# The first mixer of a hybrid two-layer network without plain float32 products, and its zero blocks written first

## The chip, the cores and the metric

One core of one Trainium2 chip runs the whole program. The metric is the device time of one execution in microseconds. The kernel before has a median of 1746.74 us over three runs.

## What is computed

Two layers on one sequence of 256 rows of width 1024, all in float32. Each layer normalises x, projects it with w_in (1024 x 5024), feeds three branches from parts of the projection, gates and merges them, projects with w_out and adds to x; then comes a feed-forward part (layer 0 dense, layer 1 with eight experts of which each row takes two).

```python
h = rmsnorm(x, norm_mix[layer])
z = h @ w_in[layer]
cq, ckv, kpe, u_ssm, conv_a, conv_g, gates = jnp.split(z, IN_OFFSETS, axis=-1)
y_attn = mla_branch(cq, ckv, kpe, ...) @ w_o_attn[layer]
s = jax.nn.gelu(s5_branch(u_ssm, ...))
s = s * jax.nn.sigmoid(s @ ssm_w_glu[layer] + ssm_b_glu[layer])
y_ssm = s @ w_o_ssm[layer]
y_conv = conformer_conv_branch(conv_a, conv_g, ...) @ w_o_conv[layer]
g = jax.nn.sigmoid(gates).reshape(B, L, 3, D)
merged = g[:, :, 0] * y_attn + g[:, :, 1] * y_ssm + g[:, :, 2] * y_conv
x = x + merged @ w_out[layer]
```

## The kernel before, in words

**Weights and products.** Weights come from memory in units of 1 MB on SyncE's queue (`load_next`, two raw buffers) and are used in pieces of 128x1024. A piece holds the 128x128 blocks of eight products. `top_up` makes a piece ready: as a rule `split` writes a rounded high half with ScalarE (L198, `bwh`) and the difference as a low half with VectorE (L199, `bwl`), three buffers of each. `mm3` then does a product in three passes, high x high (L211), high x low (L212), low x high (L213), with the activations split in the same way (`aH`, `aL`). A piece whose key is "native" is handed on unsplit, and `mm3` does one product in plain float32 (L209), with unsplit activations (`h`, written by eight ScalarE copies, L737, in `to_hT`).

**The order of the first mixer.** A plan for each layer, a string in `CFG`, lists the projections (u, cq, conv, gate, ...) and, after a "+", the lanes that begin there (the tables of the state-space branch, its scan `ssm_gen`, the attention, the norm of the convolution). A "!" marks a native projection. Between the pieces `tick` gives the lanes their turns from a budget of VectorE time; each split takes 1.13 from it, each piece done adds to it (3.4 if native, otherwise 2.6). So fewer native pieces also move the lanes' steps in the order. A scheduler then fixes the order on each engine, except on GpSimd, which follows the program text.

**Names at the places that the change touches.** `setup` loads x and makes the identity; `feature_rows` loads nine small vectors (norm gains, biases), the first two on SyncE's queue and the other seven on GpSimd's; `rms` squares x on ScalarE (L668, `junk`) and makes nr, the inverse root, on VectorE (L133 and L136); `norm_stats` scales x to xn (L710, L711); L728 are the transposes. `ssm_tiles` makes the blocks mout0, mout1, bx with zeros around their content and writes the zeros with GpSimd (L537), `ssm_inp` does so for toep (L594). In the state-space branch rn and ab are blocks of coefficients, P (two tiles, hr and hi in the code) are the states after the scan, L1185 to L1187 the products of y with toep and mout, L1259 the transposes of ys in `ssm_act`, which then updates u (through lt). `cacc` is the sum of the convolution's taps, rr the inverse root of its norm, L762 spreads rr over rows, and br is the branch output that w_o_conv multiplies.

```python
if native:
    self.ready.append((key, src, None))
else:
    self.budget -= 1.13
    self.ready.append((key,) + self.wsplit(src))
```

Of the kernel before, what the change touches and what calls it, by code (L numbers as in the profile page):

```python
# [8 lines left out]
F32 = mybir.dt.float32  # L9
# [13 lines left out]
NCH = 16  # L23
# [14 lines left out]


CFG = dict(  # L40
    plans=("u0 u1! cq0 +out conv0! +in gate2! +tables +ssm ckv0 gate4! +norm gate0 gate5 gate7! conv1 "
           "qkv0 +attn gate6 glu0 ossm0 gate1 oattn0 gate8 ossm1 +cln gate3 gatea gateb oattn1 gate9 "
           "oconv0 oconv1",
           "u0 u1 +ssm gate5 cq0 conv0 gate6 gate7 ckv0 +norm gate4! glu0 conv1 qkv0 +attn ossm0 gate2 "
           "gate0 ossm1 gate1 gate8 +cln gatea oattn0 gate9 gate3 oattn1 gateb oconv0 oconv1"),
    rate=(1.0, 1.3), cap=(7.0, 3.0, 1.5), frate=0.85, native=("glu", ""), acc=("sc o b c", "b c sc o"),
    ngate=5, nraw=2, nwp=3, ns=3, wps="w w w aH",
    raw2="E mout0 mout1 U+v toep q cqk+zc k br br lc", raw3="bx+u mt,ys+P0,P1")

# [32 lines left out]
class Prog:  # L82
# [259 lines left out]
    def setup(self):  # L342
        nc, io = self.nc, self.io
        cp = self.cp = self.pool("const")
        self.mixp = self.pool("mix")
        self.nraw, self.nwp = CFG["nraw"], CFG["nwp"]
        self.raws, self.turn = [("raw", self.nraw)] * self.nraw, 0
        self.dr = self.pool("dr", space=bass.MemoryType.DRAM)
        self.x = cp.tile([128, 2, D], F32, name="x")
        for t in range(2):  # L350
            nc.sync.dma_start(self.x[:, t, :], io["x"][0, t * 128:(t + 1) * 128, :])
        self.ident = cp.tile([128, 128], F32, name="ident")
        make_identity(nc, self.ident)
        self.ones = cp.tile([128, 128], F32, name="ones")
        nc.vector.memset(self.ones, 1.0)
        self.lc, self.lc_at = self.mixp.tile([128, 2048], F32, name="lc", bufs=1), 0
        self.cmask = self.const(256)
        nc.gpsimd.memset(self.cmask, 0.0)
        nc.gpsimd.affine_select(self.cmask[:, 128:], self.cmask[:, 128:], pattern=[[-1, 128]],
                                compare_op=OP.is_ge, fill=-3.0e38, base=0, channel_multiplier=1)  # L360


    def feature_rows(self):
        nc, io = self.nc, self.io
        spec = [("norm_mix", 8), ("norm_ffn", 8), ("q_norm", 2), ("kv_norm", 1), ("ssm_d", 4),
                ("ssm_b_glu", 4), ("conv_b", 4), ("conv_ln_g", 4), ("conv_ln_b", 4)]
        rows = [self.mixp.tile([128, 128], F32, tag=t, name="frows", bufs=1) for t in ("wr", "P1")]
        self.col = {}
        r = 0
        for name, n in spec:  # L370
            first = r < 32
            (nc.sync if first else nc.gpsimd).dma_start(
                rows[0][r:r + 2 * n] if first else rows[1][r - 32:r - 32 + 2 * n],
                io[name].rearrange("l (c p) -> (l c) p", p=128))
            for l in range(DEPTH):
                self.col[name, l] = r + l * n
            r += 2 * n
        self.nf = r
        self.fv = self.cp.tile([128, r], F32, name="fv")
        return rows  # L380
# [149 lines left out]
    def ssm_tiles(self):  # L530

        wk = self.mixp
        self.mout = [wk.tile([128, NCH, Q, 2, 16], F32, name=f"mout{i}", bufs=1) for i in range(2)]
        self.bx = wk.tile([128, 2, 4, Q, 2, 16], F32, name="bx", bufs=1)
        self.E = wk.tile([128, 2, NCH, NQ], F32, name="E", bufs=1)
        for t in (self.bx, *self.mout):
            self.nc.gpsimd.memset(t, 0.0)  # L537


# [46 lines left out]
    def ssm_inp(self, l, ps):  # L586
        nc, io, wk = self.nc, self.io, self.mixp
        c0 = 16 * l
        c0m = self.c0m
        sh = [128, Q, 16, 16]  # L590
        flat = lambda v: v.rearrange("p k c o -> p (k c o)")
        self.minT = [wk.tile([128, NCH, 128], F32, tag=t, name="minT", bufs=1) for t in "qk"]
        toep = self.toep = wk.tile([128, NCH, 128], F32, name="toep", bufs=1)
        nc.gpsimd.memset(toep, 0.0)  # L594
        z = wk.tile([128, 2048], F32, tag="br", name="pz", bufs=2)
        tmp = z[:, :1024].rearrange("p (k c o) -> p k c o", k=Q, c=16)
        b = z[:, 1024:1536].rearrange("p (i c o) -> p i c o", i=2, c=16)
        for i, nm in enumerate(("ssm_b_re", "ssm_b_im")):
            nc.scalar.dma_start(b[:, i], io[nm][l].rearrange("(c g) p i -> (g p) c i", g=2))
        ab = wk.tile([128, 2, Q, 16, 16], F32, tag="br", name="ab", bufs=2)  # L600
        fr, fi = (self.bp[:, i].rearrange("p (k c) -> p k c", k=Q)[:, :, c0:c0 + 16, None].to_broadcast(sh) for i in range(2))
        br, bi = (b[:, i][:, None].to_broadcast(sh) for i in range(2))
        for o, x, y, op in ((0, br, bi, OP.subtract), (1, bi, br, OP.add)):
            self.tt(ab[:, o], fr, x, OP.mult)
            yield 1.1
            self.tt(tmp, fi, y, OP.mult)
            yield 1.1
            self.tt(flat(ab[:, o]), flat(ab[:, o]), flat(tmp), op)
            yield 1.1
        fx = lambda v: v.rearrange("p k g i -> p (k g i)")  # L610
        for u in range(4):
            cs = slice(4 * u, 4 * u + 4)
            for i in range(2):
                for d in range(2):
                    hp = slice(64 * d, 64 * d + 64)
                    nc.scalar.activation(self.bx[hp, i, :, :, d], ab[hp, i, :, cs].rearrange("p k c o -> p c k o"),
                                         AF.Copy)
            for i in range(2):
                p = self.spare(ps)
                for j in range(4):  # L620
                    nc.tensor.transpose(p[:, j * 128:(j + 1) * 128], fx(self.bx[:, i, j]), self.ident)
                nc.scalar.activation(self.minT[i][:, cs].rearrange("p a b -> p (a b)"), p, AF.Copy)
            p = self.spare(ps)
            for j in range(4):
                for i in range(2):
                    nc.tensor.matmul(p[:, 32 * j:32 * j + 32], fx(self.bx[:, i, j]),  # L626
                                     c0m[:, i, 4 * u + j].rearrange("p a b -> p (a b)"), start=(i == 0), stop=(i == 1))

            nc.scalar.activation(self.toep[:, cs, 96:], p[:, :128].rearrange("p (c m) -> p c m", c=4), AF.Copy)
            yield 0.5  # L630
        for st in range(Q - 1):
            for k in range(st + 1):
                o = 32 * (k + Q - 1 - st)
                nc.scalar.activation(self.toep[o:o + 32, :, 32 * st:32 * st + 32],
                                     self.toep[32 * k:32 * k + 32, :, 96:], AF.Copy)
        yield 0
# [223 lines left out]
    def mixer(self, l, wk, psp):  # L860
        nc, io = self.nc, self.io
# [435 lines left out]

        if l == 0:
            self.conv_params(psp)
            self.ssm_tiles()  # L1300
        lanes = dict(tables=lambda: self.ssm_tables(l), out=lambda: self.ssm_out(l, psp),
                     norm=attn_norm, attn=attn_gen, ssm=ssm_gen, cln=conv_ln)
        lanes["in"] = lambda: self.ssm_inp(l, psp)
# [2 lines left out]
        for tok in self.plan[l]:  # L1306
# [5 lines left out]
            t, e = tok.rstrip("!"), "!" * tok.count("!")  # L1312
            name, i = t[:-1], int(t[-1], 16)
# [600 lines left out]
```

## Time and profile before

| what | value |
|---|---|
| runs | 1746.73, 1746.74, 1750.08 us; median 1746.74 |
| profiled execution | 1745.99 us, span 1744.3 us |
| granted TensorE clock | 0.992 of full speed |
| TensorE (PE) busy | 1695.3 us, 97% |
| VectorE (DVE) busy | 1466.3 us, 84% |
| ScalarE (ACT) busy | 1169.5 us, 67% |
| GpSimd (POOL) busy | 48.5 us, 3% |

The span lies between the first and the last instruction of the profiled execution; 1.7 us of its time lie around it. The mixer of layer 0, which the change touches, ends at about 275 us of the span.

### The profile page before, as it was taken

The numbers are of one execution on the slowest core, as the hardware profiler recorded it, in microseconds if no ns is written. First come the engines' busy times: TensorE is split into PE (matmuls) and PEld (weight loads), VectorE is DVE, ScalarE is ACT, GpSimd is POOL, SyncE is SP. The second block draws the span as 40 slices with busy tenths as digits, with TensorE's granted clock in tenths as the row PEclk, the third lists the DMA queues.
The fourth block names the chain that finished last, engine by engine and source line by source line (L and its number), as shares of the span: only waits on it lengthen the run. The fifth ranks groups of instructions, "written<-read, shape, count | busy, mean of one in ns | idle before, by whom it ended". The sixth has DMA issues, their size and how long they took to land.

```text
span 1744.3 us, 26025 instructions
## 1 busy us (share of the span) xinstructions
PE 1695.3 (97%) x9687; PEld 1459.0 (84%) x9687; DVE 1466.3 (84%) x2150; ACT 1169.5 (67%) x1534; POOL 48.5 (3%) x71
## 2 busy tenths in 40 slices
PE   6999999999989999999999999999999999999997
PEld 5899898999979989978888888888788888888875
DVE  7878887855558997689999999989898988998897
ACT  4545555664453565567888887777777877878785
POOL 3000000000000000000000000000000000100020
PEclk9999999999999999989999999999999999999998
DMA  5433355545643756769999899799999899898993
GB/s 156 128 103 98 99 182 191 171 145 186 194 145 116 236 163 218 259 219 382 374 366 393 292 341 398 268 394 396 337 394 394 305 393 395 326 394 326 396 394 141
DMA packets 261899, 471.27 MB, mean 270 GB/s; under 512 B 26932, under 2 KB 104916, under 8 KB 261764
## 3 DMA queue, kind: packets, MB, share of 16 engines
q1 hardware_dynamic: 244580, 455.69, 73.2%
q0 software_dynamic: 2544, 8.06, 1.3%
q10 hardware_dynamic: 14640, 5.77, 1.3%
q8 instruction: 78, 1.28, 0.3%
q14 instruction: 57, 0.47, 0.1%
HBM read 463.70 MB, written 5.78 MB: 269 GB/s over the span
## 4 chain that ended last, share of the span: by engine, by line
PE 90%; DVE 5%; ACT 3%; DMA 2%; issue 1%; ACTq 0%; SPq 0%; DVEq 0%
PE mm L212 18%; PE mm L211 18%; PE mm L213 18%; PE Y L212 6%; PE Y L213 6%; PE Y L211 6%; PE acc L213 2%; PE acc L212 2%; PE acc L211 2%; PE mm L209 2%; PE tr L1709 1%; DVE bwl L199 1%; PE bu L1176 1%; PE spare L626 1%; ACT bwh L198 1%
## 5 line engine op out<-in xcount | busy, mean ns | idle before, releaser
L199 DVE TENSOR_TENSOR bwl<-braw,bwh 128x1024 fp32r<-128x1024 f32 x246 | 298.6, 1222 | 112.0 <-ACT bwh L198 103.9
L198 ACT ACTIVATE bwh<-braw 128x1024 fp32r<-128x1024 f32 x246 | 258.9, 1058 | 198.5 <-PE mm L212 121.8
L211 PE MATMUL mm<-bwh,bxm 128*128 128x512 f32 x672 | 266.1, 396 | 0.0
L212 PE MATMUL mm<-bwl,bxm 128*128 128x512 f32 x672 | 264.6, 394 | 1.2 <-DVE bwl L199 1.2
L213 PE MATMUL mm<-bwh,bxm 128*128 128x512 f32 x672 | 262.6, 391 | 0.0
L212 PEld LDWEIGHTS mm<-bwl,bxm 128*128 128x128 f32 x672 | 126.3, 188 | 33.5 <-DVE bwl L199 9.4
L211 PE MATMUL mm<-aH,bwh 128*128 128x256 f32 x528 | 153.1, 291 | 0.5 <-ACT bwh L198 0.5
L213 PE MATMUL mm<-aH,bwl 128*128 128x256 f32 x528 | 150.5, 285 | 1.4 <-DVE bwl L199 1.4
L212 PE MATMUL mm<-aL,bwh 128*128 128x256 f32 x528 | 150.6, 285 | 0.0
L213 PEld LDWEIGHTS mm<-bwh,bxm 128*128 128x128 f32 x672 | 126.1, 188 | 25.8
L211 PEld LDWEIGHTS mm<-bwh,bxm 128*128 128x128 f32 x672 | 126.3, 188 | 25.2
L212 PE MATMUL Y<-bwl,bgates 128*128 128x512 f32 x336 | 133.5, 397 | 0.8 <-DVE bwl L199 0.8
L213 PE MATMUL Y<-bwh,bgates 128*128 128x512 f32 x336 | 132.8, 395 | 0.0
L211 PE MATMUL Y<-bwh,bgates 128*128 128x512 f32 x336 | 122.5, 400 | 0.0
L136 DVE SCALAR_TENSOR_TENSOR cacc<-zc,lc,cacc 128x256 f32<-128x256 f32 x240 | 108.0, 478 | 3.4 <-ACT cacc L966 2.3
L211 PEld LDWEIGHTS mm<-aH,bwh 128*128 128x128 f32 x528 | 101.6, 193 | 4.1 <-issue 2.2
L213 PEld LDWEIGHTS mm<-aH,bwl 128*128 128x128 f32 x528 | 101.5, 192 | 1.8 <-DVE bwl L199 1.6
L212 PEld LDWEIGHTS mm<-aL,bwh 128*128 128x128 f32 x528 | 101.6, 192 | 0.2
L212 PE MATMUL mm<-fL,bwh 128*128 128x256 f32 x352 | 99.3, 282 | 0.0
L213 PE MATMUL mm<-fH,bwl 128*128 128x256 f32 x352 | 99.3, 282 | 0.0
L211 PE MATMUL mm<-fH,bwh 128*128 128x256 f32 x352 | 99.3, 282 | 0.0
L213 PE MATMUL mm<-baH,bxm 128*128 128x512 f32 x224 | 87.7, 392 | 0.0
(427 smaller groups left out, 4201.5 us busy)
## 6 DMA issues: line engine op xcount, KB each, us to landing
bmout<-in_moe_w SPq DMA_DIRECT2D x46, 1024.0 KB, 10.6
bbr<-in_moe_w SPq DMA_DIRECT2D x44, 1024.0 KB, 14.0
braw<-in_moe_w SPq DMA_DIRECT2D x44, 1024.0 KB, 14.2
braw<-in_w_in SPq DMA_DIRECT2D x38, 1024.0 KB, 5.4
braw<-in_ffn_w SPq DMA_DIRECT2D x31, 1024.0 KB, 5.4
bE<-in_moe_w SPq DMA_DIRECT2D x23, 1024.0 KB, 10.5
btoep<-in_moe_w SPq DMA_DIRECT2D x23, 1024.0 KB, 13.0
bq<-in_moe_w SPq DMA_DIRECT2D x23, 1024.0 KB, 14.2
```

What stands on the lines that cost most here:

```text
L136: self.nc.vector.scalar_tensor_tensor(out, a, s, b, op0=op0, op1=op1)
L198: i = nc.scalar.activation(h, src, AF.Copy)
L199: j = nc.vector.tensor_tensor(l, src, h.bitcast(F32), op=OP.subtract)
L209: mm(out, wh, xh, start=start, stop=stop, skip_group_check=True)
L211: mm(out, wh, xh, start=start, stop=False, skip_group_check=True)
L212: mm(out, wh, xl, start=False, stop=False, skip_group_check=True)
L213: self.lastmm = mm(out, wl, xh, start=False, stop=stop, skip_group_check=True).ins
L626: nc.tensor.matmul(p[:, 32 * j:32 * j + 32], fx(self.bx[:, i, j]), c0m[:, i, 4 * u + j].rearrange("p a b -> p (a b)"), start=(i == 0), sto ...
L1176: nc.tensor.matmul(pb[:, i, c], self.minT[i][:, pair_at(8 * h + c)], U[:, 8 * h + c], start=True, stop=True)
L1709: nc.tensor.transpose(p[:, q * 128:(q + 1) * 128], s[:, q * 128:(q + 1) * 128], self.ident)
```

## The change

Four things are done. The "!" is taken from all projections of layer 0 (u1, both parts of conv0, gates 2, 4 and 7), and "glu" from the native keys of layer 0, so that 14 pieces more are split and 112 products more go in three passes; the one native projection of layer 1 (gate4) stays. `ssm_tiles` is called in `setup`, right behind the identity, and also makes and clears toep of layer 0, in the order mout0, mout1, bx, toep. The last seven small vectors of `feature_rows` are loaded from ScalarE's queue. With no native piece in layer 0, the eight ScalarE copies of h go, and the output of the state-space branch is split for the product with the glu weights (two splits of 128x512 more).

```diff
--- before.py
+++ after.py
@@ -38,12 +38,12 @@
 
 
 CFG = dict(
-    plans=("u0 u1! cq0 +out conv0! +in gate2! +tables +ssm ckv0 gate4! +norm gate0 gate5 gate7! conv1 "
+    plans=("u0 u1 cq0 +out conv0 +in gate2 +tables +ssm ckv0 gate4 +norm gate0 gate5 gate7 conv1 "
            "qkv0 +attn gate6 glu0 ossm0 gate1 oattn0 gate8 ossm1 +cln gate3 gatea gateb oattn1 gate9 "
            "oconv0 oconv1",
            "u0 u1 +ssm gate5 cq0 conv0 gate6 gate7 ckv0 +norm gate4! glu0 conv1 qkv0 +attn ossm0 gate2 "
            "gate0 ossm1 gate1 gate8 +cln gatea oattn0 gate9 gate3 oattn1 gateb oconv0 oconv1"),
-    rate=(1.0, 1.3), cap=(7.0, 3.0, 1.5), frate=0.85, native=("glu", ""), acc=("sc o b c", "b c sc o"),
+    rate=(1.0, 1.3), cap=(7.0, 3.0, 1.5), frate=0.85, native=("", ""), acc=("sc o b c", "b c sc o"),
     ngate=5, nraw=2, nwp=3, ns=3, wps="w w w aH",
     raw2="E mout0 mout1 U+v toep q cqk+zc k br br lc", raw3="bx+u mt,ys+P0,P1")
 
@@ -351,6 +351,7 @@
             nc.sync.dma_start(self.x[:, t, :], io["x"][0, t * 128:(t + 1) * 128, :])
         self.ident = cp.tile([128, 128], F32, name="ident")
         make_identity(nc, self.ident)
+        self.ssm_tiles()
         self.ones = cp.tile([128, 128], F32, name="ones")
         nc.vector.memset(self.ones, 1.0)
         self.lc, self.lc_at = self.mixp.tile([128, 2048], F32, name="lc", bufs=1), 0
@@ -369,7 +370,7 @@
         r = 0
         for name, n in spec:
             first = r < 32
-            (nc.sync if first else nc.gpsimd).dma_start(
+            (nc.sync if first else nc.scalar).dma_start(
                 rows[0][r:r + 2 * n] if first else rows[1][r - 32:r - 32 + 2 * n],
                 io[name].rearrange("l (c p) -> (l c) p", p=128))
             for l in range(DEPTH):
@@ -533,7 +534,8 @@
         self.mout = [wk.tile([128, NCH, Q, 2, 16], F32, name=f"mout{i}", bufs=1) for i in range(2)]
         self.bx = wk.tile([128, 2, 4, Q, 2, 16], F32, name="bx", bufs=1)
         self.E = wk.tile([128, 2, NCH, NQ], F32, name="E", bufs=1)
-        for t in (self.bx, *self.mout):
+        self.toep = wk.tile([128, NCH, 128], F32, name="toep", bufs=1)
+        for t in (*self.mout, self.bx, self.toep):
             self.nc.gpsimd.memset(t, 0.0)
 
 
@@ -590,8 +592,9 @@
         sh = [128, Q, 16, 16]
         flat = lambda v: v.rearrange("p k c o -> p (k c o)")
         self.minT = [wk.tile([128, NCH, 128], F32, tag=t, name="minT", bufs=1) for t in "qk"]
-        toep = self.toep = wk.tile([128, NCH, 128], F32, name="toep", bufs=1)
-        nc.gpsimd.memset(toep, 0.0)
+        if l:
+            self.toep = wk.tile([128, NCH, 128], F32, name="toep", bufs=1)
+            nc.gpsimd.memset(self.toep, 0.0)
         z = wk.tile([128, 2048], F32, tag="br", name="pz", bufs=2)
         tmp = z[:, :1024].rearrange("p (k c o) -> p k c o", k=Q, c=16)
         b = z[:, 1024:1536].rearrange("p (i c o) -> p i c o", i=2, c=16)
@@ -1297,7 +1300,6 @@
 
         if l == 0:
             self.conv_params(psp)
-            self.ssm_tiles()
         lanes = dict(tables=lambda: self.ssm_tables(l), out=lambda: self.ssm_out(l, psp),
                      norm=attn_norm, attn=attn_gen, ssm=ssm_gen, cln=conv_ln)
         lanes["in"] = lambda: self.ssm_inp(l, psp)
```

Three places of the order, each before and after. First VectorE in the tables of the state-space branch (pz, rn and ab are its blocks of coefficients, c0m a small matrix, cacc the convolution's taps, `bwl` a low half of a weight piece). Before:

```order
L127 TENSOR_TENSOR rn<-pz,lc 128x1024 x2
L136 SCALAR_TENSOR_TENSOR c0m<-aux,lc 128x512
L127 TENSOR_TENSOR pz<-pz,lc 128x1024
L127 TENSOR_TENSOR rn<-rn,pz 128x1024
L127 TENSOR_TENSOR pz<-pz,lc 128x1024
L136 SCALAR_TENSOR_TENSOR rn<-rn,pz 128x1024
L136 SCALAR_TENSOR_TENSOR zc<-mt,zc 128x2x256
L136 SCALAR_TENSOR_TENSOR cacc<-zc,lc,cacc 128x256 x5
L127 TENSOR_TENSOR ab<-lc,pz 128x1024
L136 SCALAR_TENSOR_TENSOR cacc<-zc,lc,cacc 128x256
L199 TENSOR_TENSOR bwl<-braw,bwh 128x1024 x2
```

After (another `bwl` stands eight rows ahead of the first one shown; five short rows and two cacc lie between):

```order
L136 SCALAR_TENSOR_TENSOR c0m<-aux,lc 128x512
L127 TENSOR_TENSOR lc<-scr 128x32
L127 TENSOR_TENSOR pz<-pz,lc 128x1024
L127 TENSOR_TENSOR rn<-pz,lc 128x1024 x2
L127 TENSOR_TENSOR rn<-rn,pz 128x1024
L136 SCALAR_TENSOR_TENSOR cacc<-zc,lc,cacc 128x256
L127 TENSOR_TENSOR pz<-pz,lc 128x1024
L136 SCALAR_TENSOR_TENSOR cacc<-zc,lc,cacc 128x256
L136 SCALAR_TENSOR_TENSOR rn<-rn,pz 128x1024
L136 SCALAR_TENSOR_TENSOR cacc<-zc,lc,cacc 128x256
L199 TENSOR_TENSOR bwl<-braw,bwh 128x1024
```

The same operations stand in both, in nearly the same order; before, TensorE works on plain products meanwhile and the next `bwl` pair comes behind the first ab, while now these rows lie between one `bwl` and the next, and each piece that TensorE uses needs one.

Second, VectorE at the end of the scan of h = 1 (P as above, u and lt of the update in `ssm_act`, sm of the softmax). Before:

```order
L127 TENSOR_TENSOR P_1602<-wr,E 128x512
L127 TENSOR_TENSOR P_1603<-wr,E 128x512
L127 TENSOR_TENSOR P_1602<-P_1602,T_1604 128x512
L127 TENSOR_TENSOR P_1603<-P_1603,wi 128x512
L136 SCALAR_TENSOR_TENSOR u<-u,fv,aux 128x256 x2
L1118 ISA sm,st<-sc,lc 128x128
```

After:

```order
L127 TENSOR_TENSOR P_1827<-wr,E 128x512
L127 TENSOR_TENSOR T_1829<-wi,E 128x512
L136 SCALAR_TENSOR_TENSOR u<-u,fv,aux 128x256 x2
L127 TENSOR_TENSOR P_1827<-P_1827,T_1829 128x512
L127 TENSOR_TENSOR P_1828<-wr,E 128x512
L136 SCALAR_TENSOR_TENSOR lt<-lt,u 128x512
L127 TENSOR_TENSOR wi<-wi,E 128x512
L1121 ISA sm,st<-sc,lc 128x128
L1121 ISA st 128x1
L136 SCALAR_TENSOR_TENSOR u<-lt,u 128x512
L127 TENSOR_TENSOR P_1828<-P_1828,wi 128x512
```

Both P were whole ahead of the update of u; the second P is now finished behind it.

Third, TensorE at the end of the convolution's norm (aux spreads rr; br is a branch output, aH the normed input). Before, where br is still that of the attention:

```order
L211 MATMUL mm<-br,bwh 128x256
L212 MATMUL mm<-br,bwh 128x256
L762 MATMUL aux<-ident,rr 128x128 [waits DVE_49,PE_49]
L762 MATMUL aux<-ident,rr 128x128
L213 MATMUL mm<-br,bwl 128x256
L211 MATMUL mm<-br,bwh 128x256
L212 MATMUL mm<-br,bwh 128x256
L213 MATMUL mm<-br,bwl 128x256
```

After, where br is that of the convolution:

```order
L211 MATMUL mm<-aH,bwh 128x256
L212 MATMUL mm<-aL,bwh 128x256
L765 MATMUL aux<-ident,rr 128x128 [waits DVE_49,PE_49]
L765 MATMUL aux<-ident,rr 128x128
L213 MATMUL mm<-aH,bwl 128x256
L211 MATMUL mm<-br,bwh 128x256 [waits PE_49,Activation_49]
L211 MATMUL mm<-br,bwh 128x256 [waits Activation_49]
L212 MATMUL mm<-br,bwh 128x256 [waits DVE_49]
```

Before, 88 rows lie between the spreading of rr and the first product with the convolution's br; after, one row does.

## Rows read from the trace of the kernel before

**Rows 1.** The page, busy time of each engine.

```profile
PE 1695.3 (97%) x9687; PEld 1459.0 (84%) x9687; DVE 1466.3 (84%) x2150; ACT 1169.5 (67%) x1534; POOL 48.5 (3%) x71
```

**Rows 2.** Stretch 16 to 270 us: length, busy of PE, PEld, DVE, ACT, POOL; clock, DMA.

```profile
16.00:270.00 254.00, 249.65 (x1839) 228.35 (x1840) 217.39 (x575) 134.10 (x252) 4.26 (x8) 1.00 0.43 125
```

**Rows 3.** What TensorE waited for, 16 to 290 us: total, times, longest.

```profile
PE hp L728 <- ACT xn L710: 8.3, 1, 8.3
PE mm L213 <- DVE bwl L199: 1.4, 1, 1.4
```

**Rows 4.** Timeline, 0 to 30 us: start, duration, engine, line, operation [idle before].

```profile
0.81 1.28 ACT L668 ACT_TABLE_LOAD   x1 [0.81 <-PEq L1903]
...
4.52 20.53 SPq L768 DMA_DIRECT2D braw<-in_w_in  x3
4.53 0.63 ACT L668 ACTIVATE junk<-x 128x512 f32<-128x512 f32 x1 [2.43 <-DMA x<-in_x]
...
5.12 0.52 POOL L372 DMA_DIRECT2D frows<-in_conv_ln_b  x1
...
7.89 0.96 POOL L537 MEMSET bx<- 128x1024 f32 x1
...
8.11 0.16 DVE L136 SCALAR_TENSOR_TENSOR nv<-ss 128x2 f32<-128x2 f32 x1 [0.98 <-ACT junk L668]
8.30 5.90 DVE L133 TENSOR_SCALAR nr<-nv 128x2 int32<-128x2 int32 x1
...
14.06 0.12 POOL L644 MEMSET E<- 128x16 f32 x1
...
15.81 1.01 DVE L711 TENSOR_SCALAR xn<-x,nr 128x256 f32<-128x256 f32 x3
...
17.90 1.05 ACT L198 ACTIVATE bwh<-braw 128x1024 fp32r<-128x1024 f32 x1
...
24.06 0.52 ACTq L554 DMA_DIRECT2D pz<-in_ssm_c_re  x1
```

**Rows 5.** DMA issues, 0 to 20 us: queue, count, KB each, median us to landing.

```profile
braw<-in_w_in SPq DMA_DIRECT2D x2, 1024.0 KB, 7.0
...
frows<-in_q_norm POOLq DMA_DIRECT2D x1, 2.0 KB, 4.3
```

**Rows 6.** Groups by line, 0 to 300 us: count, busy, mean ns, idle before.

```profile
L209 PE MATMUL mm<-h,braw 128*128 128x256 f32 x192 | 44.1, 381 | 0.0
...
L209 PE MATMUL mm<-u,braw 128*128 128x256 f32 x32 | 7.6, 386 | 0.0
...
L199 DVE TENSOR_TENSOR bwl<-braw,bwh 128x1024 fp32r<-128x1024 f32 x57 | 69.5, 1221 | 19.8 <-ACT bwh L198 19.2
```

**Rows 7.** Timeline of TensorE, plain and three-pass products, 51 to 70 us.

```profile
51.76 12.68 PE L209 MATMUL mm<-h,braw 128*128 128x256 f32 x58
...
67.14 0.28 PE L211 MATMUL mm<-aH,bwh 128*128 128x256 f32 x1
...
69.89 0.28 PE L213 MATMUL mm<-aH,bwl 128*128 128x256 f32 x1
```

**Rows 8.** Timeline of VectorE, 50 to 72 us.

```profile
57.14 1.23 DVE L136 SCALAR_TENSOR_TENSOR rn<-rn,pz 128x1024 f32<-128x1024 f32 x1
...
65.64 2.35 DVE L199 TENSOR_TENSOR bwl<-braw,bwh 128x1024 fp32r<-128x1024 f32 x2
```

**Rows 9.** Timeline at the scan of h = 1, 155 to 168 us.

```profile
157.79 2.46 PE L1259 MATMUL aux<-ys,ident 128*32 128x128 f32 x32
...
158.74 0.68 DVE L127 TENSOR_TENSOR P<-P,wi 128x512 f32<-128x512 f32 x1
...
160.29 0.87 DVE L136 SCALAR_TENSOR_TENSOR u<-u,fv,aux 128x256 f32<-128x256 f32 x2 [0.88 <-PE aux L1259]
```

**Rows 10.** Timeline at the end of the convolution, 238 to 256 us.

```profile
244.07 1.65 DVE L136 SCALAR_TENSOR_TENSOR cacc<-cacc,fv,aux 128x256 f32<-128x256 f32 x4
...
247.58 0.76 DVE L199 TENSOR_TENSOR br<-lt,br 128x256 fp32r<-128x256 f32 x2
```

## The prediction

> **What bounds the kernel now.** I read the busy times first, then the stretches of the first mixer, then TensorE's waits, then single rows at the places that the change touches. The busy row [rows 1] shows TensorE at work 97% of the span, so a microsecond saved counts only where TensorE saves it or waits less. The second engine is VectorE with 84%. In the mixer of layer 0 the reader should look at one stretch, 16 to 270 us [rows 2]: TensorE is busy 249.65 of 254.00 us, VectorE 217.39. TensorE loses 4.35 us there, VectorE has 36.6 us free. The waits [rows 3] say the same: the longest wait of TensorE in the whole mixer is the one before its first transpose, 8.3 us; after it the longest is 1.4 us, for the low half of a weight. So in this stretch TensorE sets the end, with VectorE some 14% behind. In the order of instructions everything from the product with w_out of layer 0 on stands alike in both kernels, on every engine; a shift up to there, whatever its sign, reaches the end at its full size as long as TensorE stays the bound afterwards, which 97% says it is.
>
> **Part 1: the start.** The row to see is the DVE instruction that makes nr from nv: 128x2 elements, and it takes 5.90 us, from 8.30 to 14.20 [rows 4]; its neighbour of the same size takes 0.16. GpSimd's memsets begin at 7.89 and the last ends at 14.18, the same moment: nr was held while GpSimd worked. The scaling xn begins 1.61 us after nr's end, at 15.81, and TensorE starts at 16.37. The change takes seven DMA issues from GpSimd (0.52 us each in the row shown, so 3.6 us), which it had ahead of those memsets; the memsets themselves and the rest remain, in another order. GpSimd is quiet at about 14.2 - 3.6 = 10.6. Against that, ScalarE now issues the seven DMAs ahead of its table load. An issue on its queue takes 0.52 us [rows 4], so six of them end at 0.8 + 3.1 = 3.9; the seventh waits until the first has landed, 4.3 us after its issue on the other queue [rows 5], so 5.1, and ends at 5.6; the table load (1.28) ends at 6.9. The first square then starts at 6.9, where it started at 4.53 before. From there to nr were 3.77 us, 0.6 of them a wait for the second half of x, which will have landed: nr starts at 10.1. Held to 10.6 and 0.16 long, it lets xn start at 12.2 to 12.4, against 15.81. I take **-3.5 us**. Bounds: if GpSimd no longer holds nr, -4.0. On the other side stands SyncE: each of its small loads now waits for an earlier landing, and the first weights wait for the sixth DMA of ScalarE, issued at about 3.4 and landed some 4.3 later. They are issued at 7.7 in place of 4.52, take 7.0 us [rows 5], and are there at 14.7; the first split, at 17.90 before [rows 4], wants them at 14.4. A landing 1 us past that makes the term -2.5. ScalarE's table load could hide less, or nothing be gained; this is a rival below.
>
> **Part 2: the products.** 112 products in plain float32 become three-pass products: the plain groups have 192 + 32 rows [rows 6], two rows to a product. The price of each comes from rows back to back [rows 7]: 58 plain rows in 12.68 us are 0.2186 a row, 0.437 a product; 23 rows of the three-pass kind from 67.14 to 69.89 are 0.1196 apart, 0.359 a product. The gain is 112 x 0.078 = **-8.7 us** of TensorE. The rows leave little doubt about this term: -8.5 to -9.
>
> [...]
>
> **Part 3: what the splits cost.** 14 more weight pieces are split. One split takes VectorE 1.22 us [rows 6] and two more 128x512 splits of u some 0.6 each: 14 x 1.13 (two back to back take 2.35 [rows 8], the second 1.13 more) + 1.2 = 17.0 us, in a stretch in which VectorE had 36.6 us free. ScalarE gets 14 copies of about 1 us and loses eight smaller ones; it was busy 134.10 of 254.00 us [rows 2], so I put it at nothing, hidden beside the products, and if that cover went each copy would cost its 1 us. On VectorE most of it hides too, since TensorE needs 24 rows x 0.12 = 2.9 us for a piece and VectorE 1.13 to make one. It does not hide in three places where the order puts something else ahead of what TensorE waits for.
>
> *The tables of the state-space branch.* Between two splits VectorE now has six operations of 128x1024 elements, one with c0m, five taps and six short ones. A big one takes 1.23 [rows 8], a tap 0.4 (four cacc in 1.65 [rows 10]), c0m 0.6, a short one 0.2: 7.4 + 2.0 + 0.6 + 1.2 = 11.2 us. With three buffers TensorE has at most 3 x 2.9 = 8.6 us of stock when this begins. With full stock the wait is 11.2 + 1.2 - 8.6 = 3.8, with two pieces 6.7. The kernel before has the same operations under plain products, and pays 1.4 for a low half here [rows 3]. So the place costs 2.4 to 5.3 more; I take **+2.6**, near the full stock, as VectorE makes a piece faster than TensorE uses it up to there.
>
> *The second half of the scan (h = 1, the products P of its y).* Before, both P stood ahead of the update of u on VectorE and were ready as TensorE ended the transposes of ys [rows 9], the last row of P and then u; the y products follow without a wait. Now the second P ends behind u, lt and the second u. From the end of the transposes: u 0.87, then P, P, lt and wi at 0.6 each back to back (0.68 alone [rows 9]), a softmax maximum 0.3, u and the last P 0.6 each: 4.8 us, and the step through ScalarE's tanh fits in beside it. TensorE has 0.4 us of other rows. **+4.4 us**; bounds 0 (if other work on VectorE already delays the transposes by as much) and 5.5.
>
> *The end of the convolution.* Before, 88 rows of TensorE (10.6 us) lie between the transposes of rr and the first product with w_o_conv, and the chain cacc, tanh, lt, br hides under them. Now one row does. The chain in rows [rows 10]: four cacc 1.65, lt 0.4, one weight split 1.13 that stands ahead in VectorE's order, one br 0.4 (two take 0.76), and some 0.3 to start: 3.9 us to the first low half. The other three br follow every 1.2 us, for 1.1 us of products each. I take **+4.0**; bounds 2.5 (the split not in the way) and 6.
>
> **The sum.** -3.5 - 8.7 + 2.6 + 4.4 + 4.0 = -1.2 us, against the profiled execution's own 1745.99: 1744.8. The median of the runs, 1746.74, is 0.75 above that execution, so the forecast is 1745.5. About 0.2%, 3.5 us, is what a measurement here can tell from no change; the forecast is no difference.
>
> **Rivals.**
> A: *the waits stay hidden.* For it: before, TensorE lost only 4.35 us with VectorE 86% busy [rows 2], and the three buffers even out small delays; a wait at one place lets VectorE run ahead for the next. Against it: the places at the scan and the convolution are chains that begin with a TensorE result, which no stock shortens. If only a quarter of Part 3 shows, the sum is -3.5 - 8.7 + 2.7 = -9.5: 1737.
>
> B: *VectorE becomes the bound; slower.* Its 217.4 us become 234.4. If its idle time, 36.6 us before, recurs because it comes from its own waits for ScalarE and TensorE (the low halves alone wait 19.8 us, mostly for the high half, up to 300 us [rows 6]), the stretch lasts 271.0, 17.0 more; less 3.5 at the start, +13.5: 1760. It decides, that is, the kernel is slower by over 3.5 us, where VectorE takes in less than 10.0 of the added 17.0 us in its idle time. For it: a stretch of 251 us would need VectorE at 93% or more. Against: TensorE lost only 4.35 us in that stretch [rows 2], so little of VectorE's idle time came with a shortage of its results. A half-way case gives 1753.
> [...]
>
> C: *the start gives nothing.* ScalarE's seven issues, the queued small loads and the late first weights together eat the 3.5 us. For it: no row shows DMA issues ahead of the table load or the lane waits of SyncE. Against: GpSimd's quiet comes 3.6 us earlier in any case. Time: 1745.5 + 3.5 = 1749.
>
> That the change does not do what it says is out: in the order of the changed program the first mixer has no plain product left; layer 1 keeps its 16.
>
> **Chances.** The forecast 0.45, A 0.20, B 0.20, C 0.15. Of the forecast's 0.45 I count 0.15 as faster by over 0.2% (waits at their lower ends), 0.27 as no difference, 0.03 as slower. A is faster. B is slower; C is 0.13 no difference, 0.02 slower. Together faster 0.35, same 0.40, slower 0.25. The range runs from 1737, the time of A, to 1755, just above the half-way case of B; the full B and what lies below A are left out. The forecast's own range, by the bounds of its terms, is 1739 to 1752.
>
> **What would show it.** In the profile after: nr takes well under 1 us and xn starts near 12.3; L209 is gone from the first 270 us; the low halves' L199 group there counts 14 more; TensorE's waits list P at the y products (about 4), br or aux at the convolution (about 4), and a low half near 50 to 65 us. It is wrong if these waits do not add up to more than about 5 us (A), or if TensorE's losses sit spread over many short waits for bwl, with VectorE over 90% busy and TensorE below 93% in 16 to 270 us (B), or if xn starts no earlier than 15 (C).

## The result

The changed kernel takes 1774.3 us (median of four runs, 1772.52 to 1775.56), the kernel before 1747.43: a ratio of 1.0151, 95% interval 1.0139 to 1.0163. It is slower by 27 us, where I had forecast no difference and a range up to 1755.

The page's busy row, which answers to [rows 1]:

```profile
PE 1715.3 (97%) x9799; PEld 1470.2 (83%) x9799; DVE 1478.7 (83%) x2166; ACT 1182.4 (67%) x1542; POOL 40.7 (2%) x64
```

TensorE is busy 20 us longer, though the products that went to three passes should have made it 8.7 us shorter. The table by stretches, from the first transpose to the first product with w_out (columns as in [rows 2]), for the changed kernel:

```profile
11.09:279.92 268.83, 250.34 (x1929) 233.38 (x1930) 225.81 (x581) 143.84 (x255) 4.24 (x8) 0.96 0.40 120
```

and for the kernel before:

```profile
16.37:264.95 248.58, 244.60 (x1817) 224.18 (x1817) 212.17 (x568) 130.46 (x247) 4.26 (x8) 1.00 0.42 124
```

The mixer begins 5.3 us earlier and ends 15.0 later, so it is 20.3 us longer: 14.5 of them TensorE idle (18.49 against 3.98 us) and 5.7 TensorE busy. The mean granted clock (third value from the end) is 0.96 there, 1.00 before. Another 12 us are lost behind the mixer, evenly from 800 us on, in the expert part, where both kernels have the same instructions in the same order; the same product there takes longer (before: 266.1 us busy, 396 ns each). In its row the second name, bxm, is the weight block (128*128), and the first what is streamed (512 columns):

```profile
L211 PE MATMUL mm<-bwh,bxm 128*128 128x512 f32 x672 | 269.6, 401 | 0.0
```

The start, which answers to [rows 4]:

```profile
3.18 0.28 ACTq L373 DMA_DIRECT2D frows<-in_conv_ln_b  x1
...
4.78 0.63 ACT L671 ACTIVATE junk<-x 128x512 f32<-128x512 f32 x1
...
7.63 0.85 DVE L424 COPY scr<-scr 32x128 f32<-32x128 f32 x1 [6.42 <-DMA scr<-in_ssm_log_dt]
7.64 1.05 SPq L771 DMA_DIRECT2D braw<-in_w_in  x2
7.67 0.58 POOL L447 MEMSET scr<- 128x1 f32 x16
...
8.47 0.23 DVE L136 SCALAR_TENSOR_TENSOR nv<-ss 128x2 f32<-128x2 f32 x1
...
8.73 0.19 DVE L133 TENSOR_SCALAR nr<-nv 128x2 int32<-128x2 int32 x1
...
10.53 1.01 DVE L714 TENSOR_SCALAR xn<-x,nr 128x256 f32<-128x256 f32 x3
```

nr takes 0.19 us in place of 5.90, and xn starts at 10.53 in place of 15.81. TensorE's waits in the mixer, which answer to [rows 3]:

```profile
PE mm L213 <- DVE bwl L199: 3.9, 1, 3.9
PE mm L211 <- ACT br L198: 3.0, 2, 2.5
PE y L1190 <- DVE st L131: 2.8, 1, 2.8
PE spare L624 <- ACT bx L619: 1.5, 2, 1.3
PE aux L560 <- DVE lc L136: 1.2, 1, 1.2
PE y L1189 <- DVE P L127: 1.2, 1, 1.2
PE mm L211 <- ACT lt L1286: 1.1, 1, 1.1
```

The three places of the prediction are all here: the low half (`bwl`) in the tables, P and st at the scan, and br, of whose 3.0 us the 2.5 stand at the end of the convolution and 0.5 at the attention's output. The 1.1 for lt stand at the glu products. The place at the scan of h = 1 in the timeline (compare [rows 9]):

```profile
157.87 0.87 DVE L136 SCALAR_TENSOR_TENSOR u<-u,fv,aux 128x256 f32<-128x256 f32 x2 [2.08 <-PE aux L1262]
...
159.40 0.43 PE L1189 MATMUL y<-P,mout 128*128 128x63 f32 x2 [1.20 <-DVE P L127]
...
161.88 0.68 DVE L127 TENSOR_TENSOR P<-P,wi 128x512 f32<-128x512 f32 x1
...
162.62 0.69 PE L1190 MATMUL y<-P,mout 128*128 128x63 f32 x2 [2.79 <-DVE st L131]
...
166.51 0.63 PE L1190 MATMUL y<-P,mout 128*128 128x63 f32 x2
```

The wait is 1.20 + 2.79 us (the second ends with the second P, at 162.56; st is only the VectorE row nearest to its end). Behind it the y products come in pairs 0.43 us apart (0.22 ahead of it), and the stretches there show why:

```profile
156.00:160.00 4.00, 2.63 (x32) 2.16 (x28) 2.13 (x5) 0.63 (x1) 0.00 (x0) 1.00 0.01 4
160.00:164.00 4.00, 1.38 (x7) 1.38 (x7) 4.00 (x13) 2.08 (x5) 0.00 (x0) 0.54 0.00 0
164.00:168.00 4.00, 4.00 (x20) 4.00 (x20) 3.32 (x10) 1.07 (x4) 0.00 (x0) 0.50 0.00 0
168.00:172.00 4.00, 4.00 (x21) 4.00 (x21) 0.00 (x0) 0.00 (x0) 0.46 (x1) 0.50 0.00 0
```

TensorE is idle most of 158 to 162.6, the granted clock falls at 160.3, within this gap, from 1.00 to 0.50, the only two values in this trace's record and in that of the kernel before, and stays there to about 177, for 15 us of work.

### The profile page after: what moved, and what is told of

The parts are those of the page before. It is cut to its first block, busy times and chain, and to the rows that moved or that the text cites. A ratio compares the mean times of both kernels' runs of the same rounds, so it can differ in the third digit from the quotient of the medians.

```text
span 1772.8 us, 26281 instructions
## 1 busy us (share of the span) xinstructions
PE 1715.3 (97%) x9799; PEld 1470.2 (83%) x9799; DVE 1478.7 (83%) x2166; ACT 1182.4 (67%) x1542; POOL 40.7 (2%) x64
## 4 chain that ended last, share of the span: by engine, by line
PE 89%; DVE 6%; ACT 2%; issue 1%; DMA 1%; ACTq 0%; SPq 0%; DVEq 0%
PE mm L211 19%; PE mm L212 19%; PE mm L213 18%; PE Y L212 6%; PE Y L213 6%; PE Y L211 6%; PE acc L213 2%; PE acc L212 2%; PE acc L211 2%; DVE bwl L199 2%; PE tr L1711 1%; ACT bwh L198 1%; PE bu L1179 1%; PE spare L629 1%; PE aux L1262 1%
## 5 line engine op out<-in xcount | busy, mean ns | idle before, releaser
L198 ACT ACTIVATE bwh<-braw 128x1024 fp32r<-128x1024 f32 x260 | 274.2, 1059 | 234.9 <-PE mm L212 152.3
L199 DVE TENSOR_TENSOR bwl<-braw,bwh 128x1024 fp32r<-128x1024 f32 x260 | 315.9, 1222 | 114.8 <-ACT bwh L198 111.5
L211 PE MATMUL mm<-bwh,bxm 128*128 128x512 f32 x672 | 269.6, 401 | 0.0
L213 PE MATMUL mm<-bwh,bxm 128*128 128x512 f32 x672 | 265.9, 396 | 0.0
L213 PE MATMUL mm<-aH,bwl 128*128 128x256 f32 x624 | 179.7, 289 | 3.9 <-DVE bwl L199 3.9
L211 PE MATMUL mm<-aH,bwh 128*128 128x256 f32 x624 | 180.7, 290 | 0.3 <-DVE mt L136 0.3
L212 PE MATMUL mm<-aL,bwh 128*128 128x256 f32 x624 | 178.9, 287 | 0.0
L213 PEld LDWEIGHTS mm<-bwh,bxm 128*128 128x128 f32 x672 | 126.2, 188 | 29.1
L211 PEld LDWEIGHTS mm<-bwh,bxm 128*128 128x128 f32 x672 | 126.4, 188 | 28.2
L213 PE MATMUL Y<-bwh,bgates 128*128 128x512 f32 x336 | 132.8, 395 | 0.0
L213 PEld LDWEIGHTS mm<-aH,bwl 128*128 128x128 f32 x624 | 121.3, 195 | 4.9 <-DVE bwl L199 4.4
L211 PEld LDWEIGHTS mm<-aH,bwh 128*128 128x128 f32 x624 | 121.6, 195 | 2.7 <-issue 1.8
L211 PE MATMUL Y<-bwh,bgates 128*128 128x512 f32 x336 | 122.5, 400 | 0.0
L212 PEld LDWEIGHTS mm<-aL,bwh 128*128 128x128 f32 x624 | 121.6, 195 | 0.2
L213 PE MATMUL mm<-fH,bwl 128*128 128x256 f32 x352 | 100.5, 286 | 0.0
L211 PE MATMUL mm<-fH,bwh 128*128 128x256 f32 x352 | 99.4, 282 | 0.0
L211 PE MATMUL mm<-baH,bxm 128*128 128x512 f32 x224 | 88.6, 396 | 0.0
## 6 DMA issues: line engine op xcount, KB each, us to landing
bE<-in_moe_w SPq DMA_DIRECT2D x23, 1024.0 KB, 10.5
btoep<-in_moe_w SPq DMA_DIRECT2D x23, 1024.0 KB, 14.4
```

The costliest lines, as they stand in the source:

```text
L198: i = nc.scalar.activation(h, src, AF.Copy)
L199: j = nc.vector.tensor_tensor(l, src, h.bitcast(F32), op=OP.subtract)
L211: mm(out, wh, xh, start=start, stop=False, skip_group_check=True)
L212: mm(out, wh, xl, start=False, stop=False, skip_group_check=True)
L213: self.lastmm = mm(out, wl, xh, start=False, stop=stop, skip_group_check=True).ins
```

## The experiments

Two costs had no place in the prediction: the slower expert part and the clock. The first four runs separate the parts.

**1. Same program, xm at another place.** With no plain product in layer 0, the tile h (tag xm) is no longer requested early; its tag is first requested by a later tile, and everything with that tag, the experts' input bxm among it, lies at byte 214784 of a partition in place of 58592 (the places are the built program's). An early request that is never written brings it to 95456.

```diff
-        h32 = hp.tile([128, KD, L], F32, tag="xm", name="h32", bufs=1) if whole else None
+        h32 = hp.tile([128, KD, L], F32, tag="xm", name="h32", bufs=1) if whole or l == 0 else None
```

> The changed kernel, with the tile of tag xm requested in the first mixer as the kernel before does it, but never written there; the order of instructions is the same on every engine, only places in SBUF differ (xm at byte 95456 of a partition in place of 214784). Theory 1 (the place of xm makes the expert products slower): the 128x512 products that stream bxm fall from 401/399/396 ns back to about 396/394/391, the time falls by about 12 us to 1762, and the first 280 us stay as in the changed kernel. Rival 1a (the expert part is slower for another reason, the chip or the shifted start): no change, 1774.

Measured: 1762.99 us (1761.87 to 1768.81), 11.3 less than the changed kernel; the first row of the group is back:

```profile
L211 PE MATMUL mm<-bwh,bxm 128*128 128x512 f32 x672 | 266.1, 396 | 0.0
```

**2. The reverse in the kernel before**: all large tiles requested up front, in the changed kernel's order (30 tags; the first and the last two stand here).

```diff
+        for t, n, b in (("mout0", 2048, 1),
...
+                        ("ys", 512, 1), ("xm", 2048, 1)):
+            for _ in range(b):
+                self.buf(t, n, F32, b)
```

> The kernel before, with all large tiles requested up front in the order of the changed kernel, so that xm lies at byte 214464 in place of 58592; the order of instructions is the same. Theory 1: the bxm products rise to about 401/399/396 ns and the time by about 12 us to 1759, all of it after 800 us. Rival 1a: 1747, as before.

Measured: 1758.79 us, ratio 1.0065 (1.0048 to 1.0081), 11.4 us more than the kernel before with not one instruction moved. Theory 1 stands from both sides; rival 1a falls.

**3. The start alone**: `ssm_tiles` in `setup` and the queue as in the change, plans and native keys as before; against the changed kernel:

```diff
-    plans=("u0 u1 cq0 +out conv0 +in gate2 +tables +ssm ckv0 gate4 +norm gate0 gate5 gate7 conv1 "
+    plans=("u0 u1! cq0 +out conv0! +in gate2! +tables +ssm ckv0 gate4! +norm gate0 gate5 gate7! conv1 "
...
-native=("", "")
+native=("glu", "")
```

> The kernel before with only the zero blocks written first and the seven small loads on ScalarE's queue; layer 0 keeps its plain products and xm its early request. Theory 2 (the start itself is a gain of 5.3 us, nothing later gives it back): xn starts at about 10.5 and the time is 1747.4 - 5.3 = 1742. Rival 2a (the gain is lost in the mixer because VectorE's tables or weights aren't ready earlier): 1746 to 1748.

Measured: 1743.35 us, ratio 0.9972 (0.9961 to 0.9984). Theory 2 holds for the larger part: xn starts at 10.53, and 4.1 us of the 5.3 arrive at the end.

**4. The three-pass products alone**: the changed plans and keys, xm requested early as in the first experiment, and the start as before; against the changed kernel:

```diff
-        self.ssm_tiles()
...
-            (nc.sync if first else nc.scalar).dma_start(
+            (nc.sync if first else nc.gpsimd).dma_start(
```

> The kernel before with only the plain products of layer 0 made three-pass ones, start and queues as before, and xm requested early so that it keeps its place. Theory 3 (the three-pass mixer itself costs 20 us: 11 to 12 of waits and 16 to 17 by TensorE's clock at its lower level after the waits, against 8.7 gained): about 1767. Rival 3a (the loss in the mixer comes from the early start, which shifts what meets what): 1738 to 1750.

Measured: 1767.84 us, ratio 1.0117 (1.0101 to 1.0134), 20.4 us more. So the loss in the mixer doesn't need the early start. The three parts add up nearly to the whole: -4.1 + 20.4 + 11.3 = 27.6 us, and the whole change costs 26.9.

**5 and 6. Is it the wait, or the clock behind it?** Both start from the first experiment's kernel (1762.99 us). One puts 32 useless products into the wait; the other writes the update of u (`ssm_act(0, Y)`) behind both P, in front of the y products. If the clock goes to 0.50 because TensorE sits idle there, either should keep it at 1.00, with the pairs of y products 0.22 us apart in place of 0.43.

```diff
                     nc.tensor.matmul(y[:, j, 1:], mo(0, c), hr[:, j, :NQ - 1], start=False, stop=False)
+                    if l == 0 and h == 1 and j == 0:
+                        for _ in range(32):
+                            nc.tensor.matmul(y[:, 7], self.toep[:, pair_at(c)], U[:, c], start=True, stop=True,
+                                             skip_group_check=True)
```

```diff
+                if l == 0 and h == 1:
+                    ssm_act(0, Y0[0])
...
-            ssm_act(0, Y)
...
+            Y0.append(Y)
+            if l:
+                ssm_act(0, Y)
```

> The changed kernel with xm requested early (1763 us), and 32 useless 128x64 products into a part of y that is written anew later, queued on TensorE between the first product with the first P and the one with the second P of h = 1, where it waits 2.8 us. [...]

> The changed kernel with xm requested early (1763 us), and the update of u for h = 0 written behind the making of both P of h = 1, so that VectorE finishes the second P ahead of it but for one half of u. Theory 4 (the wait costs itself, 4.0 us, and about 7 more by the clock that falls behind it): the wait for P shrinks to 1 or 2 us, the clock stays up, and the time falls by 8 to 11 us to 1752 to 1755. Rival 4a (VectorE is the bound here, so another wait takes its place): less than 3 us, above 1760.

Measured: 1759.78 us with the useless products, 1755.53 with both P first. The 32 products showed as 64 rows of 0.11, 7.1 us, and so put off the second P's products by 4.2 us; the pairs of y products behind them came 0.22 us apart, as at a clock of 1.00, and the median still fell by 3.2, though one of its four runs lies above all of the first experiment's. With both P first the wait for P was 0.6 us, the clock there stayed at 1.00, and 7.5 us went, just short of the 8 expected, while the wait at the convolution's end grew from 2.5 to 3.4 us.

**7 and 8. What about the place of a tile?** Both start from the early start (1743.35 us) and add nothing but 32 unused bytes, before and behind xm, or before the gates tiles. The second's edit:

```diff
+            if not hasattr(self, "pad"):
+                self.pad = wk.tile([128, 8], F32, name="pad", bufs=1)
             gates[i] = wk.tile([128, 2, L], F32, name="gates", bufs=self.ngate)
```

> The kernel before with the early start (1743.4 us), and 32 bytes of nothing in front of xm and 32 behind it, so that only xm moves against the 64-byte grid, from 95456 (32 past a multiple of 64) to 95488 (a multiple). Theory 5 (what counts for a weight block is its place against 64 bytes; a multiple is the slow one): the products with bxm rise from 0.228 to 0.233 us apart, 12 us more, 1755. Rival 5a (what counts is how high in the partition it lies): no change, 1743.

> The kernel before with the early start (1743.4 us), and 32 bytes of nothing in front of the gates tiles, which moves them and what lies above by 32 bytes, from 206528 (a multiple of 64) to 206560. Theory 5: the products with bgates fall from 0.233 to 0.228 us apart; 2016 less 672 of them have gates as weight block, 1344 x 0.005 = 7 us less, 1736. Rival 5a: no change, 1743.

Measured: 1751.66 us with xm on a multiple of 64 bytes, 1735.77 with the gates 32 past one (ratio to the kernel before 0.9943, 0.9927 to 0.9960). The groups, with xm moved (401 ns, where the fast ones have 396), then the gates before and after their move:

```profile
L211 PE MATMUL mm<-bwh,bxm 128*128 128x512 f32 x672 | 269.6, 401 | 0.0
```

```profile
L213 PE MATMUL Y<-bwh,bgates 128*128 128x512 f32 x336 | 132.8, 395 | 0.0
```

```profile
L213 PE MATMUL Y<-bwh,bgates 128*128 128x512 f32 x336 | 131.0, 390 | 0.0
```

Theory 5 holds and rival 5a falls: xm stayed low in the partition and became slow, the gates stayed high and became fast. With xm moved the expert part lost the 12 us expected; 4 us came back in earlier parts. The eighth kernel is the fastest of the study, 11 us below the kernel before.

**9. The wait filled exactly**: as the fifth, with 12 products.

```diff
-                        for _ in range(32):
+                        for _ in range(12):
```

> As the run with 32 useless products in the wait for the second P, but with 12 of them: a product shows as two rows 0.11 apart, so 32 of them took 7.1 us and were 4.2 us longer than the wait, while 12 take 2.7 us and just fill it. [...] Rival 4a: 1763, and the gain with 32 came from the changed order of other rows.

Measured: 1756.9 us (1753.06 to 1763.25), 6.1 less than without them; three of the four runs lie below every run without them. The stretches at the scan:

```profile
160.00:164.00 4.00, 3.89 (x35) 3.76 (x35) 4.00 (x14) 2.53 (x7) 0.00 (x0) 1.00 0.00 0
164.00:168.00 4.00, 4.00 (x42) 3.87 (x43) 1.76 (x5) 0.60 (x1) 2.13 (x4) 1.00 0.00 0
```

The same rows, from the end of the wait to the first product behind the transposes of ys, first without and then with the 12 products (L1194 there is L1190 of the other):

```profile
162.16 0.69 PE L1190 MATMUL y<-P,mout 128*128 128x63 f32 x2 [2.79 <-DVE st L131]
...
177.16 0.39 PE L211 MATMUL mm<-br,bwh 128*128 128x256 f32 x1
```

```profile
161.06 0.43 PE L1194 MATMUL y<-P,mout 128*128 128x63 f32 x2
...
169.27 0.39 PE L211 MATMUL mm<-br,bwh 128*128 128x256 f32 x1
```

The wait is as long as it was, only filled with nothing useful, and the clock stays at 1.00: 15.0 us of work become 8.2, so between 6 and 7 us are the clock's.

**10 and 11. The start in halves**, from the kernel before: the first is the third experiment's kernel with the queue put back, the second the kernel before with one line changed.

```diff
-            (nc.sync if first else nc.scalar).dma_start(
+            (nc.sync if first else nc.gpsimd).dma_start(
```

```diff
-            (nc.sync if first else nc.gpsimd).dma_start(
+            (nc.sync if first else nc.scalar).dma_start(
```

> The kernel before with only the zero blocks written first; the seven small loads stay on GpSimd's queue, behind the blocks. Theory 2a (nr is held only while large memsets run on GpSimd, not by its other work): nr starts near 8.3 and takes 0.2 us, xn starts near 10.1, and the time is 5 to 6 us below the kernel before, 1741. Rival 2b (nr waits until GpSimd is quiet, as I predicted): GpSimd is busy until about 13, xn starts near 14 and the gain is under 2 us.

> The kernel before with only the seven small loads moved to ScalarE's queue; the zero blocks stay where they are. GpSimd's large memsets then run from about 4.3 to 10.4 us. Theory 2a: nr starts near 8.5 and is held to about 10.5, xn starts near 12.1, the gain is about 3.7 us, 1743. If the queue alone were what matters (rival 2c), the gain would be the 4 us of both together.

Measured: 1744.26 us with the zero blocks alone (ratio 0.9984, 0.9974 to 0.9993), 1752.93 with the queue alone (1.0032, 1.0017 to 1.0048). With the blocks first, nr takes 0.17 us while GpSimd still issues DMAs,

```profile
7.68 0.74 POOL L373 DMA_DIRECT2D frows<-in_q_norm  x1
...
8.37 0.17 DVE L133 TENSOR_SCALAR nr<-nv 128x2 int32<-128x2 int32 x1
```

so rival 2b, my prediction, falls. The gain is 3, not 5 to 6: in the profiled execution, 2 us above the median, the lead is 4.1 us at the mixer's end and gone by 700 us. What spends it is not shown. The queue alone went against the expectation, 5.7 us slower. TensorE does start 2.5 us earlier; VectorE is now held in another instruction, while the large memsets run from 4.3 to 10.5:

```profile
7.83 2.87 DVE L423 COPY scr<-scr 32x128 f32<-32x128 f32 x1 [6.61 <-DMA scr<-in_ssm_log_dt]
```

and at the scan of h = 1 this kernel, too, waits 1.0 us for P, and the clock is low behind it:

```profile
168.00:172.00 4.00, 4.00 (x20) 4.00 (x20) 0.00 (x0) 0.40 (x1) 1.20 (x1) 0.50 0.00 0
```

In its profiled execution, 4 us above the median, it loses 4 to 5 us on the kernel before from its start to the scan and 6 more there; no run separates these losses.

**12. A small part of the change on the fastest kernel**: only the glu products in three passes (the "!" kept).

```diff
-native=("glu", "")
+native=("", "")
```

> The fastest kernel so far (early start, gates 32 bytes higher, 1735.8 us) with only the 16 glu products of layer 0 in three passes: 2 more weight splits and 2 splits of u. Theory 3 (what a three-pass product costs is the split of u and of the weights on the way to it, not the products): 1.2 us are gained on TensorE, and the split of the second half of u, 0.6 on ScalarE and 0.7 on VectorE, now stands between u and the glu products: between no change and 3 us slower, 1736 to 1739. Rival 3b (a small part of the change pays): 1734.5.

Measured: 1741.52 us against 1735.77, 5.8 us slower and outside both expectations. The split of u shows as one wait of 0.9 us and is not the main cost: in the profiled executions (the twelfth's is 4 us above its median) both kernels are level up to the scan and 7 us apart at 204 us. The order at the scan changes here too (the first step of the update of u now stands ahead of the last rows of both P), TensorE waits 1.2 us for P, and behind it, as read from this trace alone, the clock falls:

```profile
160.00:164.00 4.00, 4.00 (x25) 4.00 (x25) 2.28 (x7) 0.94 (x3) 0.00 (x0) 0.62 0.00 0
164.00:168.00 4.00, 4.00 (x18) 3.44 (x18) 0.43 (x4) 1.40 (x5) 2.59 (x4) 0.50 0.01 2
```

## Why the prediction was wrong

**The start** was mis-sized on the good side: -3.5 forecast, -5.3 at the first transpose, -4.1 in the time (experiment 3). One step that failed is "Held to 10.6": nr ran in 0.19 us while GpSimd was busy with small work to 10.5 us (experiments 3 and 10). The larger one is ScalarE's queue: an issue took 0.24 to 0.55 us, mostly 0.3, not 0.52, and the seventh, which waits for the first to land, went at 3.18, not at 5.1, so the squares began at 4.78, not 6.9, and nr at 8.73, not 10.1. That is 1.4 of the 1.8 us by which xn came earlier than forecast. Rival C falls.

**The products.** The rows of the three-pass kind are still 0.12 apart at a clock of 1.00, so 8.7 us may stand; no run isolates them from their splits.

**The waits** were the right ones, two of them at about their size: a low half in the tables 3.9 us (3.8 at full stock, both less the 1.4 of before), the scan 4.0 (4.4 forecast). The end of the convolution took 2.5 (4.0), its lower bound. These are 9.0 us of the 14.5 by which TensorE's idle time grew, where I had put 11.0; waits of 0.5 to 1.3 us that the prediction does not list, at bx, lc, lt, sc and bu above all, make the rest.

**What failed is the sum itself**, at two steps. First, each place was put at its wait and nothing behind it. At the scan the wait of 4.0 us was followed by 15.1 us of work at a clock of 0.50 that takes 8.2 at 1.00 (experiment 9), 6.9 us more. At the tables the clock falls too:

```profile
68.00:72.00 4.00, 4.00 (x22) 4.00 (x22) 4.00 (x6) 2.42 (x4) 0.00 (x0) 0.57 0.97 155
```

Some 17 rows are 0.21 apart there in place of 0.12, 1.6 us more. At the start, too, some 17 rows are 0.21 apart, until 20.2 us, where the kernel before has 3 or 4 such rows: about 1.3 us more. The trace's record of the granted clock begins only behind them, so this part is read from the spacing alone. Together these are 9.8 of the 14.4 us by which TensorE's busy time missed my figure. The other 4.6 are open; about 1 of them stands in single three-pass rows that are followed late (75 by over 0.14 us at 1.00 with no wait between, 7.4 us in all beyond 0.12 each; before 61, 6.6). Experiments 5, 6 and 9 show the clock's part at the scan, 6 to 7 us behind one wait for VectorE, and the prediction has no term for it; its parts at the tables and the start are read from the rows. Second, "everything from the product with w_out of layer 0 on stands alike in both kernels". The order did stand alike, and the places of the tiles did not: 11.3 us (experiments 1 and 2). The order can't show that; the built program's tile places can.

**Rival B** named the right sign, and its 1760 is near the 1763 that the change costs without the moved tile (experiment 1), but by luck: VectorE was busy 225.81 of 268.83 us, 84%, and did not become the bound. TensorE waited for single chains on VectorE and ScalarE, as part 3 has it, and the rest is clock and places. Rival A's price, a quarter of the waits, is far off.

## What to carry to other kernels

When the first request of h went, everything with its tag moved from byte 58592 to 214784, and that cost 11.3 us (experiment 1): compare the places of the tiles that TensorE loads as weight blocks before pricing a change at nothing elsewhere. A wait of TensorE is priced with what follows it, here 4.0 us at the scan with 6.9 behind it: look at the granted clock behind the waits that the kernel already has, and put work into a gap, or take the chain apart, before cutting cheap work around it. And 112 products that were 8.7 us too dear by their rows were hiding VectorE's work; where one engine's slow work covers another's, the price of removing it is in the chains of waits, not in the busy shares.

## What the runs showed of the hardware

For two tiles of this program, xm and the gates, a 128x128 weight block cost more to use when its tile began on a multiple of 64 bytes than 32 bytes past one. With 512 columns streamed, products followed at 0.233 us for xm at 214784 (the changed kernel), 214464 and 95488 (experiments 2 and 7) and the gates at 206528 (experiment 3), and at 0.227 to 0.228 for xm at 58592 (the kernel before) and 95456 (experiments 1 and 3) and the gates at 206560 (experiment 8). The mean row is 401 ns (xm, L211) and 395 (gates, L213) on the multiples, 396 and 390 past them. The blocks aH and aL, 32 past a multiple in the changed kernel and the one before, have 0.227 as well. Only xm and the gates were moved against the 64 bytes. The products whose weight block is fgh don't fit so simply (397 ns in the changed kernel, with one of its two tiles on a multiple of 64 and one not), and that is left open.

Some VectorE instructions were held for as long as GpSimd ran large memsets back to back (nr 5.90 us in the kernel before, a copy 2.87 in experiment 11). Beside GpSimd's small memsets and DMA issues nr was not (0.19 in the changed kernel, 0.17 in experiment 10), but in the changed kernel a copy that began with sixteen small memsets in a row took 0.85 us in place of 0.22. In the changed kernel the clock fell to 0.50 within a gap of 1.2 + 2.8 us, with 15 us of work at 0.50 after it, and in experiments 11 and 12 after waits of 1.0 and 1.2. Behind the 2.5 us at the convolution's end it did not fall in the changed kernel (1.00 from 268 to 272 us); in experiment 1, at the same place, it did (0.61).
